# Query low parts in both halves of 128 rows, and the retention's distance table read per layer

## The chip, the cores and the metric

The kernel runs on one core of one Trainium2 chip. The metric is the device time of one execution in microseconds (us), as the median of several runs on the chip. Before the change it is 2534.63 us (three runs, 2533.9 to 2535.16).

## The reference, cut to what matters

One inference step of a two-layer backbone. 128 context tokens and 512 latent tokens go through the same weights. Each layer has one input projection, three token mixers side by side (differential attention, retention, multi-head latent attention, "MLA"), per-channel branch gates, an output projection and a squared-ReLU MLP.

```
z = h @ w_in                                     # 1024 -> 6848 columns
dq, dk = rmsnorm(d_q), rmsnorm(d_k)              # 8 half heads of 64 columns, rope on latents
s = dq . dk * 64**-0.5; p = softmax(s); a = p[0] - lam * p[1]; oa = a @ dv
rq, rk: 4 heads of 64 columns;  o = ((rq . rk) * decay(i - j)) @ rv + (rq * decay) @ state
mq = 128 columns without position + 64 with rope;  om = softmax(mq . mk * 192**-0.5) @ mv
merged = sum_i sigmoid(g_i) * (o_i @ w_branch[i]);  x = x + g1 * (merged @ w_out)
x = x + g2 * (relu(h2 @ w_up)**2 @ w_down)
```

Three products have a contraction of only 64: the differential scores, the retention scores and the rope part of the MLA scores. They are what the change touches.

## The kernel before, in words

All activations stand with features on the 128 partitions and T = 640 tokens along the free axis. Every fp32 operand of a matrix product is split in a high part and a low part of type fp32r (`splits`, the copy rounds to the high part and a subtraction leaves the low part), and a product is done as high*high + high*low + low*high (`mm3`).

For the products with 64 rows the high and low parts of the keys are stacked: rows 0 to 63 of a tile hold the high part and rows 64 to 127 the low part (for the second head of a pair the other way round). `split2` prepares the queries for them: `Q[:, g]` gets the high part twice, in both halves of the 128 rows, and the low part goes to `ql`, rows 0 to 63 for one head of the pair and 64 to 127 for the other. A score is then two matmuls: `Q[:, g]` against the stacked keys (128 rows, high*high + high*low), and `ql` against the high half of the keys alone (64 rows, low*high). The 64-row matmuls stand in `mla_scores` (`parts`), `diff_scores` (`parts`) and `ret_head` (`score`).

In `softmax_tile` a query tile of 128 against 640 keys is done as two halves of 320 columns: for each pair of operands first the one half, then the other. So the two 64-row matmuls of a tile follow each other, and a tile of 128 context keys has one. A retention tile has one of 512 or of 128 columns.

`ql` is a buffer of the pool "f" (7 buffers of [128, 640]). The distance table `dist` [128, 896] is loaded once at the start by a DMA that POOL issues, into a tile that lives throughout; `ret_head` makes the decay matrix from it on VectorE (DVE).

The order of the work is made by a planner in the kernel itself. The main line runs through the matrix products of a layer; preparations, softmax and value products are generators on side lanes. The planner holds an estimated clock for each engine (`est`), adds an estimated delay `LAT` from one engine's end to the next engine's start, and lets a generator go on when its estimated inputs are there. `yield from need(tag=n)` makes a generator wait until n buffers of a pool are free. The instructions are then issued in that order on each engine, so every constant of the planner can move the order on every engine. `pv_ctx` is the value product of the 128 context queries: transpose, split (ScalarE/ACT copy, DVE subtraction), three matmuls. `head_out` normalises a head's output; `down`, `gemm` and `gemm_half` are the large products, in groups of 12 or 24 matmuls of 320 columns.

Of the kernel before, what the change touches and what calls it, by code (L numbers as in the profile page):

```python
# [8 lines left out]
F32 = mybir.dt.float32  # L9
# [10 lines left out]
T = 640  # L20
# [9 lines left out]
def body(ctx, tc, ins, outs):  # L30
# [7 lines left out]
    dr = ctx.enter_context(tc.tile_pool(name="dr", bufs=1, space=DRAM))  # L38


    BUFS = {"s5": 20, "kc": 5, "vx": 2, "f": 7, "t": 3, "p": 5, "pt": 2, "w": 2, "stg": 2, "kr": 1, "m": 4,
            "o": 2, "ost": 2, "g": 3, "sc": 1, "tp": 2, "pv": 1}
    PS = ("g", "sc", "tp", "pv")
    avail = dict(BUFS)
    owner = {}
# [1 line left out]


    eng = dict(pe=0.0, a=0.0, v=0.0, p=0.0, sp=0.0, dma=0.0)
    LAT = dict(pe=0.16, a=0.11, v=0.09, p=0.04, dma=0.0)  # L50
    info = {}
    rel = {k: [0.0] * n for k, n in BUFS.items()}
    fin = [0.0]
# [271 lines left out]
            eng["pe"] += 0.1  # L325
            assert n < 3000

    nmm = [0]

    def mm(out, lhsT, rhs, start, stop, beside=False):  # L330
        n = rhs.free_size()
        k = 0.14 if lhsT.shape[0] == 64 else 0.0
        est("pe", 0.02 if beside else max(0.108, n / 2400.0 + 0.0135) + k if lhsT.dtype == F32R else max(0.222, n / 600.0),
            [lhsT, rhs], [out])
        nc.tensor.matmul(out, lhsT, rhs, start=start, stop=stop)  # L335

    def mm3(out, a, b, start, stop):
# [3 lines left out]
        mm(out, al, bh, False, stop)  # L341

    def tr(out, in_, k=128):
        est("pe", 0.109, [in_], [out])
        nc.tensor.transpose(out, in_, ident[0:k, 0:k])  # L345

# [3 lines left out]
    def c_act(in_):  # L350
        return (0.051 if inps(in_) else 0.093) + in_.free_size() / 1200.0
# [3 lines left out]

    def act(out, in_, func, **kw):
        w = [out] + ([kw["accum_out"]] if "accum_out" in kw else [])
        est("a", c_act(in_) + 0.15 * ("accum_out" in kw) + 0.06 * ("bias" in kw),
            [in_] + aps(*(kw.get(k) for k in ("bias", "scale"))), w)
        nc.scalar.activation(out=out, in_=in_, func=func, **kw)  # L360

# [66 lines left out]
    bones = const.tile([128, 128], F32R, name="bones")  # L428
    ropeC = const.tile([128, 512], F32, name="ropeC")
    ropeS = const.tile([128, 512], F32, name="ropeS")  # L430
    dist = const.tile([128, 896], F32, name="dist")
    posc = const.tile([128, 4], F32, name="posc")
    decb = const.tile([128, 2, 2, 2], F32, name="decb")
    lgn = const.tile([128, 2, 2], F32, name="lgn")
# [331 lines left out]
    def split2(src, Q, ql):  # L766

        for g in range(2):
            r = slice(64 * g, 64 * g + 64)
            yield "a"  # L770
            cp(Q[r, g], src[r])
            cp(Q[64 - 64 * g:128 - 64 * g, g], src[r])
            yield "v"
            tt(ql[r], src[r], Q[r, g], SUB, "vp")

    def splitk(src, keys, c0, c1, gs=(0, 1)):

# [43 lines left out]
    def params(brow, rows, rows2):  # L821
# [12 lines left out]
        dma(ropeC, ins["const_rope"][0], "p")  # L834
        dma(ropeS, ins["const_rope"][1], "p")
        dma(posc, ins["const_posc"], "p")
        dma(dist, ins["const_dist"], "p")
        yield from until(lambda: "r" in done)
        yield from written(rows2)
        yield from need(tp=1)  # L840
# [360 lines left out]
    def pv_ctx(P, v, dst):  # L1201
        yield from need(tp=1, pt=1)
        tp = bank("tp")
        tr(tp[:, 0:128], P[:, 0:128])
        free(P)
        pt = get("pt", [128, 2, 512], F32R)
        yield from splits(tp[:, 0:128], pt[:, 0, 0:128], pt[:, 1, 0:128])
        free(tp)
        yield from need(pv=1)
        pb = bank("pv")  # L1210
        mm3(pb[:, 0:128], v, (pt[:, 0, 0:128], pt[:, 1, 0:128]), True, True)
        free(pt)
        yield "a"
        dst(pb[:, 0:128])
        free(pb)
# [8 lines left out]
    def mla_scores(hd, qn, qr, ql, R, kn, kro, V):  # L1224
# [11 lines left out]
        def parts(qt):  # L1236
            q = slice(128 * qt, 128 * qt + 128)

            def at_(c0, c1):
                kh, kl = kn.hl(c0, c1)  # L1240
                rh, _, r2 = kro.slot(a, c0, c1)
                return [(qn[:, 0, q], kh), (qn[:, 0, q], kl), (qn[:, 1, q], kh), (qr[:, a, q], r2), (ql[pp, q], rh)]
            return at_

        for st_ in range(2):
# [32 lines left out]
    def diff_scores(l, hd, q, ql, R, k, V):  # L1278
# [4 lines left out]
        def qtile(qt):  # L1283
            n = T if qt < 4 else 128
            qc = slice(128 * qt, 128 * qt + 128)
            ps_, sms = [], []
            for g in range(2):
                def parts(c0, c1):
                    kh, _, k2 = k.slot(g, c0, c1)
                    return [(q[:, g, qc], k2), (ql[64 * g:64 * g + 64, qc], kh)]  # L1290
                p, sm = yield from softmax_tile(parts, 0 if qt < 4 else 640, n, R[:, 2 * qt + g:2 * qt + g + 1])
                ps_.append(p)
                sms.append(sm)
                if g == 0:
                    rs = small(2, "st2", 4)
                    est("v", 0.08, [sms[0]], [rs[:, 0:1]])
                    nc.vector.reciprocal(rs[:, 0:1], sms[0])
                    cp(ps_[0][:, 0:n], ps_[0][:, 0:n], scale=rs[:, 0:1])
            est("v", 0.08, [sms[1]], [rs[:, 1:2]])
            nc.vector.reciprocal(rs[:, 1:2], sms[1])  # L1300
            ts(rs[:, 1:2], rs[:, 1:2], lam[:, l:l + 1])
# [61 lines left out]
        heads[br] += 1  # L1363
        heads["n"] += 1

    def ret_head(l, hd, rq, rqs, rql, rks, V, r0s, flag):
        a = hd % 2
        pp = slice(64 * a, 64 * a + 64)
        pr = hd // 2
        vof = V.of(slice(128 * a, 128 * a + 128))  # L1370

        yield from need(s5=1)
        E = s5(F32, (128, 896))
        ts(E, dist, nlb[:, l, hd:hd + 1])
# [13 lines left out]
        free(dec)  # L1388
        if a == 1:
            free(rq)  # L1390
        yield from need(pt=1)
        qds = get("pt", [128, 2, 512], F32R)
        yield from splits(qd[:, 0:512], qds[:, 0], qds[:, 1])
# [7 lines left out]
        def score(jt):  # L1401
# [4 lines left out]
            i0 = 0 if jt < 4 else 512  # L1406
            sc = bank("tp")
            mm(sc[:, 0:n], rks[:, a, j0:j0 + 128], rqs[:, a, i0:i0 + n], True, False)
            mm(sc[:, 0:n], rks[pp, a, j0:j0 + 128], rql[0][pp, i0:i0 + n], False, True)
            A = get("p", [128, T])  # L1410
            yield "v"
            e0 = 384 - j0 if jt < 4 else 384
# [100 lines left out]
    def layer(l):  # L1513
# [70 lines left out]
        for p in range(2):  # L1584
# [16 lines left out]
            def rprep(rq=rq, rk=rk, rqs=rqs, rql=rql, rks=rks, pflag=pflag, f=fin[0]):  # L1601
# [30 lines left out]
            for a in range(2):  # L1632
                def go(a=a, p=p, rq=rq, rqs=rqs, rql=rql, rks=rks, V=V, x=pflag[a]):
                    yield from until(lambda: "qk" in x and "r0" in flag and "g" in done)
                    x["r0"] = 1
                    yield from ret_head(l, 2 * p + a, rq, rqs, rql, rks, V, flag["s"], x)
                pvq.append(go())
            yield from gates(gat(l, f"R{p}"))

# [126 lines left out]
        def dq_prep(hd, raw, dst, R, f):  # L1766
# [12 lines left out]
            yield "v"  # L1779
            yield from rope(raw, q)  # L1780
            free(q)
            yield from need(f=1)
            ql = get("f", [128, T], F32R)
            state["ql", hd] = ql
            yield from split2(raw, dst, ql)
            free(raw)
# [82 lines left out]
        def qkv(p):  # L1869
# [93 lines left out]
            def rr_prep(f):  # L1963
# [2 lines left out]
                t = tt_()  # L1966
                yield from rope(rr, t)
                free(t)
                yield from need(f=1)
                qlr.append(get("f", [128, T], F32R))  # L1970
                yield from split2(rr, qr, qlr[0])
                free(rr)
                yield ""
# [438 lines left out]
```

## Time and profile before

| | |
|---|---|
| median of the runs | 2534.63 us |
| the profiled execution, its own time | 2540.84 us |
| its span, first to last instruction | 2539.0 us |
| TensorE (PE) busy | 2470.7 us, 97% of the span |
| PE weight loads (PEld) | 2354.4 us, 93% |
| VectorE (DVE) busy | 1843.4 us, 73% |
| ScalarE (ACT) busy | 1077.9 us, 42% |
| GpSimd (POOL) busy | 99.2 us, 4% |
| mean granted TensorE clock | 0.988 |

A matmul's duration in the profile contains the pipeline's filling and draining, so the durations of neighbours overlap. What a matmul costs is the distance from its start to the start of the next one; the prediction works with these distances, which a timeline shows.

### The profile page before, as it was taken

The page shows a single profiled execution, that of the slowest core. Times are in us where ns is not written, and L with a number is a line of the kernel's source. Part 1 is how long each engine was busy: PE and PEld are TensorE (multiplying, and loading weights), DVE is VectorE, ACT ScalarE, POOL GpSimd, SP SyncE. Part 2 cuts the span into 40 slices and gives each one's busy share as a digit, 9 for nine tenths or more (in the row PEclk, how much of TensorE's full clock was granted, in tenths as well). Part 3 has the DMA queues.
Part 4 walks back from the last instruction along what each step waited for, and adds up shares of the span by engine and source line. Part 5 has one row for each costly group of instructions (what it writes and reads, how often), then busy time and mean ns, then how long its engine had stood idle before and what let it go on. Part 6 is the DMA issues. An engine that isn't in the chain of part 4 may idle for free.

```text
span 2539.0 us, 40871 instructions
## 1 busy us (share of the span) xinstructions
PE 2470.7 (97%) x16468; PEld 2354.4 (93%) x16468; DVE 1843.4 (73%) x3308; ACT 1077.9 (42%) x1976; POOL 99.2 (4%) x92
## 2 busy tenths in 40 slices
PE   7999999999999999999999999999999999999999
PEld 5998998989899999999999988988888999999999
DVE  6898878888789878786477787787888764344442
ACT  5564655656523412121254556564665352112122
POOL 2000000000100000000000000000001000000000
PEclk9998999999999999999999999999999999999999
DMA  9452321214365354554233322212233522222222
GB/s 308 128 155 70 99 68 51 83 41 127 106 234 172 113 172 155 162 164 124 75 110 95 95 70 79 70 57 77 63 101 130 177 67 75 76 75 75 75 75 84
DMA packets 333261, 274.99 MB, mean 108 GB/s; under 512 B 17454, under 2 KB 290304, under 8 KB 333072
## 3 DMA queue, kind: packets, MB, share of 16 engines
q1 hardware_dynamic: 332144, 271.04, 34.3%
q8 instruction: 130, 2.13, 0.3%
q0 software_dynamic: 928, 1.34, 0.2%
q14 instruction: 59, 0.48, 0.1%
HBM read 233.73 MB, written 33.36 MB: 105 GB/s over the span
## 4 chain that ended last, share of the span: by engine, by line
PE 74%; DVE 17%; ACT 4%; issue 3%; DMA 2%; SPq 0%; POOL 0%; DVEq 0%; ACTq 0%; POOLq 0%
PE g L335 63%; PE sc L335 4%; PE pv L335 4%; DVE w L377 3%; DVE f L377 2%; PE tp L335 2%; DVE s L377 2%; PE tp L345 1%; DVE p L364 1%; ACT t L360 1%; DVE t L377 1%; DVE t L364 1%; DVE st L1156 1%; DMA s<-in_w_mod_dram 1%; DMA p<-in_w_mod_dram 1%
## 5 line engine op out<-in xcount | busy, mean ns | idle before, releaser
L335 PE MATMUL g<-s,w 128*128 128x320 f32 (+1 forms) x12432 | 1939.3, 312 | 14.5 <-DVE w L377 9.1
L335 PEld LDWEIGHTS g<-s,w 128*128 128x128 f32 (+1 forms) x12432 | 1839.2, 188 | 44.6 <-issue 19.4
L377 DVE TENSOR_TENSOR w<-stg,w 128x1024 fp32r<-128x1024 f32 (+3 forms) x308 | 342.9, 1114 | 27.7 <-ACT w L392 23.8
L392 ACT ACTIVATE w<-stg 128x1024 fp32r<-128x1024 f32 (+2 forms) x182 | 166.5, 916 | 427.6 <-PE g L335 422.2
L364 DVE SCALAR_TENSOR_TENSOR s<-g,modT,s 128x320 f32<-128x320 f32 (+2 forms) x240 | 97.8, 435 | 201.8 <-PE g L335 201.4
L394 DVE CAST w<-stg 128x1024 fp32r<-128x1024 f32 (+3 forms) x139 | 89.7, 645 | 153.3 <-PE g L335 152.8
L360 ACT ACTIVATE f<-g 128x320 f32<-128x320 f32 x136 | 59.3, 438 | 332.8 <-PE g L335 332.8
L364 DVE SCALAR_TENSOR_TENSOR p<-p,cX,p 128x640 f32<-128x640 f32 (+2 forms) x238 | 190.2, 840 | 11.1 <-DMA p<-in_w_mod_dram 11.1
L360 ACT ACTIVATE t<-t 128x640 f32<-128x640 f32 (+2 forms) x204 | 148.0, 727 | 8.6 <-DVE t L364 2.2
L335 PE MATMUL g<-w,s 128*128 128x256 f32 x1080 | 139.5, 288 | 1.0 <-ACT s L392 0.5
L392 ACT ACTIVATE f<-g 128x320 f32<-128x320 f32 x176 | 75.8, 434 | 149.8 <-PE g L335 140.2
L335 PEld LDWEIGHTS g<-w,s 128*128 128x128 f32 x1080 | 134.9, 195 | 2.4 <-ACT s L392 0.8
L335 PE MATMUL pv<-pt,s 128*128 128x256 f32 (+2 forms) x624 | 120.5, 319 | 1.8 <-DVE pt L377 1.1
L1156 DVE TENSOR_REDUCE st<-sc 128x1 f32<-128x640 f32 (+1 forms) x120 | 85.5, 713 | 35.1 <-PE sc L335 34.6
L377 DVE TENSOR_TENSOR s<-f,s 128x320 fp32r<-128x320 f32 (+3 forms) x161 | 103.9, 650 | 6.9 <-ACT s L392 3.5
L335 PEld LDWEIGHTS pv<-pt,s 128*128 128x128 f32 x624 | 92.8, 196 | 11.9 <-issue 4.7
L335 PE MATMUL sc<-s,s 128*128 128x320 f32 x384 | 78.6, 327 | 7.2 <-ACT p L360 6.0
L360 ACT ACTIVATE p<-sc,st,rd 128x640 f32<-128x640 f32 (+1 forms) x80 | 63.8, 797 | 51.2 <-DVE st L384 50.9
L392 ACT ACTIVATE s<-f 128x320 fp32r<-128x320 f32 (+3 forms) x127 | 76.9, 606 | 12.2 <-DVE f L377 8.9
L377 DVE TENSOR_TENSOR pt<-tp,pt 128x512 fp32r<-128x512 f32 (+2 forms) x112 | 61.7, 552 | 18.0 <-ACT pt L392 16.7
L335 PEld LDWEIGHTS sc<-s,s 128*128 128x128 f32 x384 | 59.7, 193 | 13.9 <-ACT p L360 9.2
L392 ACT ACTIVATE pt<-tp 128x512 fp32r<-128x512 f32 (+2 forms) x80 | 40.2, 503 | 55.9 <-PE tp L345 55.0
(280 smaller groups left out, 2242.5 us busy)
## 6 DMA issues: line engine op xcount, KB each, us to landing
stg<-in_w_in_dram SPq DMA_DIRECT2D x106, 512.0 KB, 3.8
p<-in_w_mod_dram SPq DMA_DIRECT2D x120, 320.0 KB, 4.2
stg<-in_w_up_dram SPq DMA_DIRECT2D x64, 512.0 KB, 4.2
stg<-in_w_down_dram SPq DMA_DIRECT2D x64, 512.0 KB, 3.8
gdram<-f SPq DMA_DIRECT2D x56, 320.0 KB, 2.3
f<-gdram SPq DMA_DIRECT2D x56, 320.0 KB, 4.4
stg<-in_w_branch_dram SPq DMA_DIRECT2D x24, 512.0 KB, 3.4
s<-in_w_mod_dram SPq DMA_DIRECT2D x32, 256.0 KB, 6.6
```

Source lines behind the costliest of these rows:

```text
L335: nc.tensor.matmul(out, lhsT, rhs, start=start, stop=stop)
L345: nc.tensor.transpose(out, in_, ident[0:k, 0:k])
L360: nc.scalar.activation(out=out, in_=in_, func=func, **kw)
L364: nc.vector.scalar_tensor_tensor(out=out, in0=in0, scalar=scalar, in1=in1, op0=op0, op1=op1)
L377: (nc.vector if e == "v" else nc.gpsimd).tensor_tensor(out=out, in0=in0, in1=in1, op=op)
L392: nc.scalar.activation(out=out, in_=in_, func=AF.Copy, **({} if scale is None else {"scale": scale}))
L394: nc.vector.tensor_copy(out, in_)
L1156: nc.vector.reduce_max(out=nm, in_=sv, axis=AX.XY if n == T else AX.X, negate=True)
```

## The change

In words:

- `split2` writes the low part into a tile `ql` [128, 2, T] of a new pool "q" with one buffer. For each head of the pair the low part is computed into its own half of the rows and then copied into the other half (`cp`, which takes ACT or DVE).
- The second matmul of a score then has 128 rows: `ql[:, g]` (low part twice) against the stacked keys. It computes low*high + low*low. No 64-row score matmul is left.
- Pool "f" goes from 7 to 6 buffers. The constant tile `dist` is gone; instead `r0_load` reads the table in each layer into a tile of the pool "s5" (20 buffers), by a DMA on SP's queue, and it is freed after the layer's fourth retention head.
- The planner's constants: `LAT`, the cost of `accum_out`, the cost of a matmul (a table `TURN` by the kinds of the matmul before and of this one, in place of a surcharge of 0.14 for 64 rows), and a `yield ""` in `pv_ctx` between the split and the value product.

```diff
-    BUFS = {"s5": 20, "kc": 5, "vx": 2, "f": 7, "t": 3, "p": 5, "pt": 2, "w": 2, "stg": 2, "kr": 1, "m": 4,
-            "o": 2, "ost": 2, "g": 3, "sc": 1, "tp": 2, "pv": 1}
+    BUFS = {"s5": 20, "kc": 5, "vx": 2, "f": 6, "t": 3, "p": 5, "pt": 2, "w": 2, "stg": 2, "kr": 1, "m": 4,
+            "o": 2, "q": 1, "ost": 2, "g": 3, "sc": 1, "tp": 2, "pv": 1}
...
-    LAT = dict(pe=0.16, a=0.11, v=0.09, p=0.04, dma=0.0)
+    LAT = dict(pe=0.2, a=0.146, v=0.114, p=0.12, dma=0.0)
...
+    TURN = {(0, 1): 0.098, (1, 1): 0.105, (1, 0): 0.177, (2, 0): 0.09, (2, 1): 0.09}
...
-        k = 0.14 if lhsT.shape[0] == 64 else 0.0
...
+        cost = max(0.222, n / 600.0) if kind == 2 else max(0.108, n / 2400.0 + 0.0135) + TURN.get((turn[0], kind), 0.0)
...
-        est("a", c_act(in_) + 0.15 * ("accum_out" in kw) + 0.06 * ("bias" in kw),
+        est("a", c_act(in_) + 0.235 * ("accum_out" in kw) + 0.06 * ("bias" in kw),
...
-    dist = const.tile([128, 896], F32, name="dist")
...
-            tt(ql[r], src[r], Q[r, g], SUB, "vp")
+            tt(ql[r, g], src[r], Q[r, g], SUB, "vp")
+            yield "a"
+            cp(ql[64 - 64 * g:128 - 64 * g, g], ql[r, g])
...
-        dma(dist, ins["const_dist"], "p")
...
         free(tp)
+        yield ""
         yield from need(pv=1)
...
-                return [(qn[:, 0, q], kh), (qn[:, 0, q], kl), (qn[:, 1, q], kh), (qr[:, a, q], r2), (ql[pp, q], rh)]
+                return [(qn[:, 0, q], kh), (qn[:, 0, q], kl), (qn[:, 1, q], kh), (qr[:, a, q], r2), (ql[:, a, q], r2)]
...
-                    return [(q[:, g, qc], k2), (ql[64 * g:64 * g + 64, qc], kh)]
+                    return [(q[:, g, qc], k2), (ql[:, g, qc], k2)]
...
-            mm(sc[:, 0:n], rks[pp, a, j0:j0 + 128], rql[0][pp, i0:i0 + n], False, True)
+            mm(sc[:, 0:n], rks[:, a, j0:j0 + 128], rql[0][:, a, i0:i0 + n], False, True)
...
+            yield from need(s5=1)
+            flag["dist"] = s5(F32, (128, 896))
+            dma(flag["dist"], ins["const_dist"])
...
-                yield from need(f=1)
-                rql.append(get("f", [128, T], F32R))
+                yield from need(q=1)
+                rql.append(get("q", [128, 2, T], F32R))
```

The last four lines stand likewise in `dq_prep` and `rr_prep`.

The number of matmuls is the same before and after (16206 instructions). Their order moves nearly everywhere. Two places on PE:

**Second layer, the context queries of an MLA head** (`pv_ctx`; tp is the transpose of the probabilities, pv the value product, pt their split copy, g<-s,w a large product that fills in). Before:

```order
L335 MATMUL sc2594_17807<-s52453_16965,s52467_17009 128x320 x2
L335 MATMUL sc2594_17807<-s52453_16965,f2479_17066 128x320 x2
L345 MATMUL tp2595_17820<-ident_66,p2571_17672 128x128
L335 MATMUL g2584_17751<-s51949_13573,w2532_17482 128x320 x3
L335 MATMUL pv2598_17835<-pt2596_17822,vx2433_16848 128x128 x3
```

With the change:

```order
L338 MATMUL sc2589_17800<-s52455_16989,s52469_17033 128x320 x2
L338 MATMUL sc2589_17800<-s52455_16989,q2481_17094 128x320 x2
L349 MATMUL tp2590_17811<-ident_66,p2582_17759 128x128
L338 MATMUL g2578_17738<-s51957_13618,w2534_17507 128x320 x3
L338 MATMUL g2578_17738<-s51959_13627,w2534_17507 128x320 x3
L338 MATMUL g2578_17738<-s51961_13639,w2534_17507 128x320 x3
L338 MATMUL g2595_17840<-s51935_13507,w2559_17634 128x320 x3
L338 MATMUL g2595_17840<-s51939_13529,w2559_17634 128x320 x3
L338 MATMUL g2595_17840<-s51944_13558,w2559_17634 128x320 x3
L338 MATMUL pv2600_17857<-pt2591_17813,vx2435_16872 128x128 x3
```

The value product now stands 18 large matmuls behind its transpose, before it was 3. Over the 16 such places of the program, between 3 and 16 matmuls of any kind stood between before, and 9 to 27 stand there now.

**First layer, the last retention head** (tp is here the score, s,s its first matmul and f,s or q,s its second; pv<-pt the value product). Before, from the head's first score on:

```order
L335 MATMUL tp367_2540<-s5201_1410,s5202_1411 128x512
L335 MATMUL tp367_2540<-f235_1662,s5202_1411 128x512
L335 MATMUL g364_2525<-s582_431,w355_2419 128x320 x3
L335 MATMUL g364_2525<-s587_485,w355_2419 128x320 x3
L335 MATMUL g364_2525<-s594_541,w355_2419 128x320 x3
L335 MATMUL g364_2525<-s596_545,w355_2419 128x320 x3
L335 MATMUL tp371_2566<-s5201_1410,s5202_1411 128x512
L335 MATMUL tp371_2566<-f235_1662,s5202_1411 128x512
L335 MATMUL g364_2525<-s599_576,w355_2419 128x320 x3
L335 MATMUL pv366_2536<-pt369_2551,s5225_1583 128x512 x2
```

With the change:

```order
L338 MATMUL tp378_2584<-s5198_1400,s5199_1401 128x512
L338 MATMUL tp378_2584<-q276_1945,s5199_1401 128x512
L338 MATMUL tp381_2596<-s5198_1400,s5199_1401 128x512
L338 MATMUL tp381_2596<-q276_1945,s5199_1401 128x512
L338 MATMUL pv377_2580<-pt380_2592,s5227_1587 128x512 x2
L338 MATMUL pv377_2580<-pt380_2592,s5228_1588 128x512
L338 MATMUL tp384_2611<-s5198_1400,s5199_1401 128x512
L338 MATMUL tp384_2611<-q276_1945,s5199_1401 128x512
L338 MATMUL tp387_2621<-ones_67,t373_2574 128x1 x5
L338 MATMUL pv377_2580<-pt383_2603,s5227_1587 128x512 x2
```

The fifteen large matmuls that stood between this head's first scores and its first product are no longer there.

## Rows read from the trace of the kernel before

**Rows 1.** The page's first lines and its chain of work that ended last.
```profile
span 2539.0 us, 40871 instructions
...
PE 2470.7 (97%) x16468; PEld 2354.4 (93%) x16468; DVE 1843.4 (73%) x3308; ACT 1077.9 (42%) x1976; POOL 99.2 (4%) x92
...
PE 74%; DVE 17%; ACT 4%; issue 3%; DMA 2%; SPq 0%; POOL 0%; DVEq 0%; ACTq 0%; POOLq 0%
```

**Rows 2.** PE's groups by form: rows*columns, shape, count | busy, mean ns.
```profile
L335 PE MATMUL sc<-s,f 64*128 64x320 f32 x192 | 54.1, 362 | 0.0
L335 PE MATMUL tp<-f,s 64*128 64x512 f32 x32 | 16.2, 505 | 0.0
L335 PE MATMUL sc<-kc,f 64*128 64x128 f32 x24 | 7.8, 324 | 0.0
L335 PE MATMUL tp<-f,s 64*128 64x128 f32 x8 | 2.7, 342 | 0.0
```

**Rows 3.** Timeline of PE, a differential score tile: start us, duration us, engine, operation.
```profile
1805.56 0.46 PE L335 MATMUL sc<-s,s 128*128 128x320 f32 x2
1805.95 0.55 PE L335 MATMUL sc<-s,f 64*128 64x320 f32 x2
1806.43 0.33 PE L335 MATMUL pv<-pt,vx 128*128 128x128 f32 x1
```

**Rows 4.** Timeline of PE: 65 large matmuls in a row and their successor; 512 columns; 128 columns.
```profile
1487.81 9.70 PE L335 MATMUL g<-s,w 128*128 128x320 f32 x65
1497.34 2.92 PE L335 MATMUL g<-w,s 128*128 128x256 f32 x23
...
231.04 0.86 PE L335 MATMUL pv<-pt,s 128*128 128x512 f32 x3
231.74 0.39 PE L335 MATMUL tp<-s,s 128*128 128x512 f32 x1
...
256.45 0.78 PE L335 MATMUL g<-kc,w 128*128 128x128 f32 x6
257.06 1.97 PE L335 MATMUL g<-s,w 128*128 128x320 f32 x12
```

**Rows 5.** Timeline of PE: a retention score of 512 columns, a context score of 128.
```profile
227.14 0.40 PE L335 MATMUL tp<-s,s 128*128 128x512 f32 x1
227.47 0.49 PE L335 MATMUL tp<-f,s 64*128 64x512 f32 x1
227.89 2.02 PE L335 MATMUL g<-s,w 128*128 128x320 f32 x12
...
1946.42 0.22 PE L335 MATMUL sc<-kc,s 128*128 128x128 f32 x1
1946.57 0.32 PE L335 MATMUL sc<-kc,f 64*128 64x128 f32 x1
1946.83 1.58 PE L335 MATMUL g<-s,w 128*128 128x320 f32 x9
```

**Rows 6.** PE's weight loads by form: count | busy, mean ns | idle before, what ended it.
```profile
L335 PEld LDWEIGHTS g<-s,w 128*128 128x128 f32 x12336 | 1826.9, 189 | 42.0 <-issue 18.2 <-DVE w L377 10.9 <-DVE s L377 4.5
L335 PEld LDWEIGHTS sc<-s,f 64*128 64x128 f32 x192 | 28.7, 187 | 19.0 <-issue 19.0
L335 PEld LDWEIGHTS tp<-f,s 64*128 64x128 f32 x40 | 7.5, 188 | 12.7 <-issue 12.5
```

**Rows 7.** PE's waits: us in total, times, longest.
```profile
PE pv L335 <- DVE pt L377: 7.3, 8, 1.6
```

**Rows 8.** Copies and subtractions of 64 rows by form: count | busy, mean ns.
```profile
L392 ACT ACTIVATE s<-f 64x640 fp32r<-64x640 f32 x51 | 37.5, 736 | 6.8 <-DVE f L377 6.0
L394 DVE CAST s<-f 64x640 fp32r<-64x640 f32 x21 | 10.9, 519 | 0.4
L377 DVE TENSOR_TENSOR f<-f,s 64x640 fp32r<-64x640 f32 x25 | 20.4, 815 | 0.3
```

**Rows 9.** Stretches with many heads: busy us of PE, PEld, DVE, ACT, POOL, clock, DMA share.
```profile
450.00:620.00 170.00, 164.90 (x1117) 151.17 (x1116) 146.32 (x285) 103.92 (x204) 11.84 (x10) 1.00 0.26 79
1560.00:1960.00 400.00, 383.84 (x2547) 355.62 (x2546) 323.17 (x644) 224.02 (x437) 26.89 (x22) 0.98 0.26 81
```

**Rows 10.** Timeline, first layer's last retention head: DVE's work on one score, PE's last product.
```profile
228.23 0.68 DVE L377 TENSOR_TENSOR p<-tp,s 128x512 f32<-128x512 f32 x1
228.94 0.43 DVE L394 CAST pt<-p 128x512 fp32r<-128x512 f32 x1
229.41 0.69 DVE L377 TENSOR_TENSOR pt<-p,pt 128x512 fp32r<-128x512 f32 x1
...
245.96 0.95 PE L335 MATMUL g<-w,s 128*128 128x256 f32 x3
```

**Rows 11.** Timeline, second layer's last head: normalisation on PE, last split on DVE.
```profile
1960.99 0.75 PE L335 MATMUL sc<-s,ones 128*128 128x320 f32 x4
1961.58 23.63 PE L335 MATMUL g<-s,w 128*128 128x320 f32 x160
...
1970.81 0.82 DVE L377 TENSOR_TENSOR s<-o,s 128x640 fp32r<-128x640 f32 x1
```

**Rows 12.** DMA issues: KB each, median us to landing.
```profile
dist<-in_const_dist_dram POOLq DMA_DIRECT2D x1, 448.0 KB, 7.2
```

More of the change, by code (lines that the diff above doesn't have):

```diff
@@ L326, in drive @@
             assert n < 3000
-    nmm = [0]
+    TURN = {(0, 1): 0.098, (1, 1): 0.105, (1, 0): 0.177, (2, 0): 0.09, (2, 1): 0.09}
+    turn = [0]
     def mm(out, lhsT, rhs, start, stop, beside=False):
         n = rhs.free_size()
-        k = 0.14 if lhsT.shape[0] == 64 else 0.0
-        est("pe", 0.02 if beside else max(0.108, n / 2400.0 + 0.0135) + k if lhsT.dtype == F32R else max(0.222, n / 600.0),
-            [lhsT, rhs], [out])
+        kind = 2 if lhsT.dtype != F32R else int(lhsT.shape[0] == 64)
+        cost = max(0.222, n / 600.0) if kind == 2 else max(0.108, n / 2400.0 + 0.0135) + TURN.get((turn[0], kind), 0.0)
+        turn[0] = kind
+        est("pe", 0.02 if beside else cost, [lhsT, rhs], [out])
         nc.tensor.matmul(out, lhsT, rhs, start=start, stop=stop)
@@ L343, in tr @@
     def tr(out, in_, k=128):
+        turn[0] = 2
         est("pe", 0.109, [in_], [out])
@@ L1240, in at_ @@
                 kh, kl = kn.hl(c0, c1)
-                rh, _, r2 = kro.slot(a, c0, c1)
-                return [(qn[:, 0, q], kh), (qn[:, 0, q], kl), (qn[:, 1, q], kh), (qr[:, a, q], r2), (ql[pp, q], rh)]
+                r2 = kro.slot(a, c0, c1)[2]
+                return [(qn[:, 0, q], kh), (qn[:, 0, q], kl), (qn[:, 1, q], kh), (qr[:, a, q], r2), (ql[:, a, q], r2)]
             return at_
@@ L1288, in parts @@
                 def parts(c0, c1):
-                    kh, _, k2 = k.slot(g, c0, c1)
-                    return [(q[:, g, qc], k2), (ql[64 * g:64 * g + 64, qc], kh)]
+                    k2 = k.slot(g, c0, c1)[2]
+                    return [(q[:, g, qc], k2), (ql[:, g, qc], k2)]
                 p, sm = yield from softmax_tile(parts, 0 if qt < 4 else 640, n, R[:, 2 * qt + g:2 * qt + g + 1])
@@ L1364, in head_out, with ret_head @@
         heads["n"] += 1
-    def ret_head(l, hd, rq, rqs, rql, rks, V, r0s, flag):
+    def ret_head(l, hd, rq, rqs, rql, rks, V, r0s, dists, flag):
         a = hd % 2
@@ L1370, in ret_head @@
         vof = V.of(slice(128 * a, 128 * a + 128))
+        dist = dists["dist"]
         yield from need(s5=1)
@@ L1390, in ret_head @@
             free(rq)
+        if hd == 3:
+            free(dist)
         yield from need(pt=1)
@@ L1635, in go @@
                     x["r0"] = 1
-                    yield from ret_head(l, 2 * p + a, rq, rqs, rql, rks, V, flag["s"], x)
+                    yield from ret_head(l, 2 * p + a, rq, rqs, rql, rks, V, flag["s"], flag, x)
                 pvq.append(go())
@@ L1781, in dq_prep @@
             free(q)
-            yield from need(f=1)
-            ql = get("f", [128, T], F32R)
+            yield from need(q=1)
+            ql = get("q", [128, 2, T], F32R)
             state["ql", hd] = ql
@@ L1968, in rr_prep @@
                 free(t)
-                yield from need(f=1)
-                qlr.append(get("f", [128, T], F32R))
+                yield from need(q=1)
+                qlr.append(get("q", [128, 2, T], F32R))
                 yield from split2(rr, qr, qlr[0])
```

## The prediction

> **What bounds the kernel now.** The page's first lines come first: TensorE's matmuls fill 2470.7 of 2539.0 us, and the chain of work that ended last lies on PE for 74% [rows 1]. The reader is to see that nearly every microsecond PE's queue saves can shorten the run, so long as other engines keep pace. The busy time of PE says nothing on what a single matmul costs, because neighbours overlap; for that I read starts in the timeline. 65 large matmuls of 320 columns take 1497.34 - 1487.81 = 9.53 us, 0.147 us each; three of 512 columns take 0.70, 0.233 each; six of 128 columns 0.61, 0.10 each [rows 4].
>
> **The 64-row matmuls: -44.3 us.** There are 256 of them: 192 of 320 columns, 32 of 512, 24 + 8 of 128 [rows 2].
> - A tile of 2 x 320 columns: the last 128-row pair takes 0.39 us to the first 64-row matmul, that pair 0.48 us to whatever follows [rows 3]. Four plain matmuls would be 4 x 0.147 = 0.59. The surplus is 0.87 - 0.59 = 0.285, and there are 192 / 2 = 96 such tiles: 27.4 us.
> - A retention tile of 512: 0.33 + 0.42 = 0.75 [rows 5] against 2 x 0.233 = 0.466 [rows 4]: 0.29 x 32 = 9.3 us.
> - A tile of 128: 0.15 + 0.26 = 0.41 against 0.20, so 0.21 [rows 4, 5]. I take 0.24, between this and the retention's 0.29, for 24 + 8 = 32 tiles: 7.6 us.
>
> The sum is 44.3 us. A second view bounds it: before the 64-row weight loads PE's loader stood idle for 19.0 + 12.5 us in which it waited for nothing the profile shows, and another 18.2 us before large products, many of which follow a 64-row matmul [rows 6]. So at least 31.5 and at most about 50 us. With 128 rows in the second matmul every score is an ordinary pair, and I assume it costs 0.147, 0.233 and 0.10 like the others: the matmul count does not change, and the order listing has no 64-row score left.
>
> Here a rule of the Trainium skill speaks against the change. The rows show that a 64-row matmul and its successor take longer than two 128-row ones [rows 3, 5]. The Trainium skill, TensorE: Matmul & The Clock Gate, section "Why this matters for your kernels", says that a single matmul with K = 32 takes the same time as with K = 128, and gains only by running beside others. By it the term would be 0 in place of 44.3 us; the rows of this case don't agree, so it is a rival below with a small chance.
>
> **The context value products: -6 us.** PE waited 7.3 us, 8 times, for the split copy in front of a value product [rows 7]. In the order shown, 3 large matmuls (0.44 us) stood between transpose and product before, and 18 (2.6 us) stand there now; over all 16 places at least 9 matmuls, some 1.2 us. Not all eight waits need lie at these places, so I take 6 of 7.3; the ends are 0 and 7.3.
>
> **The new copies: 0.** 16 calls of `split2` (retention 2, differential 4, MLA 2 in each layer), each with two more copies of 64x640: 32 copies of 0.74 on ACT or 0.52 on DVE [rows 8], 17 to 24 us off PE. ACT is 42% busy and DVE 73% [rows 1], and what covers them is the large products of the main line. If that cover is gone, it is the rival on `ql` below.
>
> **One buffer for `ql`: 0.** Each head's (or pair's) low part must wait until the last score of the one before has been read. Then come, for two halves of the rows, two high copies, a subtraction and the new copy: 2 x (0.74 + 0.74 + 0.82 + 0.74) = 6.1 us if one engine does all in turn [rows 8], less where ACT and DVE share. In the changed order I counted the tightest handover, the first layer's last differential head: 39 large matmuls stand between the last read of the old tile and the first of the new, 39 x 0.147 = 5.7 us [rows 4], besides 15 value products and 7 transposes. So it is covered, barely.
>
> **The work that fills moves forward, and is missed in two places.**
> - First layer, last retention head: fifteen large matmuls have left the gaps between the scores (order shown). DVE spends 0.68 + 0.43 + 0.69 = 1.8 us on each of the four 512-column scores [rows 10], while PE has 0.70 for a product and 0.47 for a score [rows 4]: 0.6 us short per score. Before, this head took from 227.14 to 245.96, 18.8 us [rows 5, 10], and stood idle in it too. I take +2 us, with ends -1 (its five 64-row matmuls are counted above) and +6.
> - Second layer, end of the mixers: before, 10.0 us passed between the end of the last head's normalising matmuls and the end of its split on DVE, under 160 large matmuls [rows 11]. In the changed order 48 stand between, and 9 more before the head's own part is read: 57 x 0.147 = 8.4 us. That leaves +1.5 us, ends 0 and +4.
>
> **The table: 0.** A DMA of 448 KB lands after 7.2 us [rows 12]. Once from POOL's queue becomes twice from SP's; in the first layer it is issued ahead of the first retention head by the whole first projection, in the second likewise behind the state's buffers. It occupies one of 20 "s5" tiles, and the order shows no head held back for it.
>
> **The planner's constants** move thousands of instructions. I give them 0 with plus or minus 8 us: PE's whole idle time is 2539.0 - 2470.7 = 68 us [rows 1], most of it in other waits that could shrink or grow.
>
> **Sum.** -44.3 - 6 + 2 + 1.5 = -46.8 us. The profiled execution took 2540.84 us, 6.2 above the median of 2534.63; the same difference against the median gives **2488 us**, -1.8%.
>
> **The rivals.**
> - *DVE becomes the bound among the heads.* It has 146.3 of 170 us in the first layer's stretch and 323.2 of 400 in the second's [rows 9]. If the 22 us saved per layer all came out of such a stretch, the first would be 148 long with 146.3 plus up to 8 copies x 0.52 = 150.5 us of DVE work. For: the numbers touch. Against: the second layer has 77 us to spare, and only part of the heads lies there. Price: half of the 64-row term, 22 us, so 2510.
> - *`ql` serialises the heads, and the run gets slower.* The place is the handover of the "q" buffer, 15 of them; it decides from 46.8 / 15 = 3.1 us of idle PE each. With all 6.1 us bare it is +92 us, 2580. For: one buffer, and planned cover of the same size as the chain. Against: the count of 39 matmuls at the tightest place.
> - *The price is not the rows'.* If a low-part matmul costs what it costs for another reason (its operand, its place behind the pair), 128 rows change nothing: 2534.6 - 6 + 3.5 = 2532. Against: 128-row matmuls of the same tiles run at plain distances within a tile, and the idle loader stands before 64-row forms alone, 0.10 us each over 192 [rows 6].
>
> **How the numbers follow.** Forecast 0.83, DVE 0.10, no change 0.04, slower 0.03. The range: down to 50 + 7.3 + 8 saved with 3.5 lost, 2473; up to the DVE case with a little on it, 2513. About 0.2% (5 us) is what a measurement of this kernel can tell from no change. Faster by more than that: the first two cases, 0.93 plus a little of the third, less what the planner's order could spoil: 0.94. Same 0.03, slower 0.03.
>
> **What would show it.** In the changed profile: no 64-row score group; a low-part pair with its successor at 0.147 us distances; the loader's idle time by "issue" down by over 30 us; PE's wait for pt before pv under 2 us; DVE's busy time up by some 10 us at most while the span falls, so its share rises to some 75%; one stretch near 200 to 240 us with PE idle behind DVE. I am wrong if 128-row low parts keep distances over 0.2 us, if waits on "q" tiles or on ACT copies take 20 us or more, or if DVE's share in the head stretches reaches 95%.

## The result, and the profile after

The changed kernel takes 2490.94 us (median of four runs, 2487.88 to 2494.18), beside 2534.27 for the kernel before on the same chip. The ratio is 0.9832, interval 0.9814 to 0.9849: 43.3 us or 1.7% faster. The forecast was 2488 us within 2473 to 2513. The total is right. But the planner's constants and the side costs of the new data path, both put at 0, were worth some 10 to 24 us each, with opposite signs; only the runs below show it.

The profiled execution took 2491.77 us. The page's first lines and its chain of work that ended last, to be read against [rows 1]:

```profile
span 2489.4 us, 40869 instructions
...
PE 2414.8 (97%) x16468; PEld 2352.9 (95%) x16468; DVE 1866.3 (75%) x3374; ACT 1069.3 (43%) x1954; POOL 77.3 (3%) x79
...
PE 74%; DVE 17%; ACT 4%; issue 2%; DMA 2%; SPq 1%; POOL 0%; DVEq 0%; ACTq 0%; POOLq 0%
```

PE remains the bound at the same 74% of the chain: its busy time fell by 55.9 us with the same 16468 matmuls. DVE has 66 instructions more, ACT 22 and POOL 13 fewer. That is more than 32 copies would bring: the planner also handed work from ACT and POOL to DVE.

PE's groups by form, the ones that answer to [rows 2]; the last number is idle time before the group and what ended it:

```profile
L338 PE MATMUL sc<-s,s 128*128 128x320 f32 x384 | 77.4, 323 | 14.7 <-ACT p L364 13.1 <-DVE t L368 1.2
L338 PE MATMUL pv<-pt,s 128*128 128x256 f32 x480 | 77.0, 286 | 5.9 <-DVE pt L381 5.7
L338 PE MATMUL sc<-s,q 128*128 128x320 f32 x192 | 44.5, 314 | 0.0
L338 PE MATMUL tp<-q,s 128*128 128x512 f32 x32 | 12.8, 400 | 0.0
L338 PE MATMUL pv<-pt,vx 128*128 128x128 f32 x48 | 8.4, 270 | 1.4 <-DVE pt L381 1.4
```

PE's weight loads by form, beside [rows 6]:

```profile
L338 PEld LDWEIGHTS g<-s,w 128*128 128x128 f32 x12336 | 1833.9, 189 | 21.7 <-DVE s L381 7.6 <-DVE w L381 3.2 <-ACT f L364 2.8
L338 PEld LDWEIGHTS sc<-s,q 128*128 128x128 f32 x192 | 33.0, 192 | 0.0
```

The low parts (`sc<-s,q`, `tp<-q,s`) now have 128 rows. The 19.0 us in which the loader stood before them without a visible reason are gone, and "issue" is no longer among the large products' first three releasers, where it was first with 18.2.

PE's waits: us in total, times, longest.

```profile
PE sc L338 <- ACT p L364: 13.6, 9, 4.0
...
PE pv L338 <- DVE pt L381: 7.6, 19, 1.3
```

The wait for the split copy pt, 7.3 us in 8 pieces before [rows 7], is 7.6 in 19 now. At the context products (`pv<-pt,vx`) it is down to 1.4 us, but it has appeared in front of the pair products (`pv<-pt,s`, 5.7 us). Before, the two forms had:

```profile
L335 PE MATMUL pv<-pt,s 128*128 128x256 f32 x480 | 79.0, 295 | 1.1 <-DVE pt L377 1.1
L335 PE MATMUL pv<-pt,vx 128*128 128x128 f32 x48 | 11.3, 296 | 6.4 <-DVE pt L377 6.3
```

The wait for a score buffer that ACT's exponential still reads leads the list with 13.6 us; it was 9.4. All of PE's waits in this view add up to 69.4 us, before to 63.2: the waits as a whole have grown.

The two places from which filling work was moved away, in the timeline of PE, beside [rows 5, 10, 11]: the first layer's last retention head, and the end of the second layer's mixers.

```profile
225.04 0.40 PE L338 MATMUL tp<-s,s 128*128 128x512 f32 x1
225.28 0.40 PE L338 MATMUL tp<-q,s 128*128 128x512 f32 x1
225.51 0.39 PE L338 MATMUL tp<-s,s 128*128 128x512 f32 x1
...
238.60 0.56 PE L338 MATMUL g<-w,s 128*128 128x256 f32 x3
...
1928.81 0.75 PE L338 MATMUL sc<-s,ones 128*128 128x320 f32 x4
1929.39 8.67 PE L338 MATMUL g<-s,w 128*128 128x320 f32 x58
1938.78 1.43 PE L338 MATMUL g<-s,w 128*128 128x320 f32 x8 [0.71 <-DVE s L381]
```

A 512-column score now stands at 0.24 and 0.23 us distances, the plain ones of [rows 4]. The head lasts 238.60 - 225.04 = 13.6 us; it lasted 18.8. Three things left it: fifteen large products (15 x 0.147 = 2.2 us), the surplus of five 64-row matmuls (4 x 0.29 + 0.24 = 1.4), and ten small `tp<-bones` products (236.00 - 234.77 = 1.2), which now stand ahead of it. Before:

```profile
234.77 1.36 PE L335 MATMUL tp<-bones,p 128*128 128x2 f32 x10 [2.22 <-DVE p L377]
236.00 1.63 PE L335 MATMUL pv<-pt,s 128*128 128x512 f32 x3
```

So PE's idle time within the head hardly changed: its busy time is 15.91 of 18.82 us in that stretch before and 11.02 of 13.56 now, which leaves 2.9 and 2.5 us. The tail waits 0.71 us behind 58 matmuls.

### The profile page after: what moved, and what is told of

Same layout as the page of the kernel before. It is cut to its first block, busy times and chain, and to the rows that moved or that the text cites. A ratio compares the mean times of both kernels' runs of the same rounds, so it can differ in the third digit from the quotient of the medians.

```text
span 2489.4 us, 40869 instructions
## 1 busy us (share of the span) xinstructions
PE 2414.8 (97%) x16468; PEld 2352.9 (95%) x16468; DVE 1866.3 (75%) x3374; ACT 1069.3 (43%) x1954; POOL 77.3 (3%) x79
## 4 chain that ended last, share of the span: by engine, by line
PE 74%; DVE 17%; ACT 4%; issue 2%; DMA 2%; SPq 1%; POOL 0%; DVEq 0%; ACTq 0%; POOLq 0%
PE g L338 64%; PE sc L338 4%; PE pv L338 3%; DVE s L381 2%; DVE w L381 2%; PE tp L338 2%; DVE p L368 1%; DVE f L381 1%; PE tp L349 1%; ACT t L364 1%; DMA s<-in_w_mod_dram 1%; DVE t L368 1%; DVE pt L381 1%; DVE st L1160 1%; SPq L160 1%
## 5 line engine op out<-in xcount | busy, mean ns | idle before, releaser
L381 DVE TENSOR_TENSOR w<-stg,w 128x1024 fp32r<-128x1024 f32 (+3 forms) x314 | 341.3, 1087 | 30.5 <-ACT w L396 26.3
L396 ACT ACTIVATE w<-stg 128x1024 fp32r<-128x1024 f32 (+3 forms) x183 | 172.2, 941 | 407.8 <-PE g L338 402.2
L396 ACT ACTIVATE s<-f 128x320 fp32r<-128x320 f32 (+3 forms) x109 | 64.1, 590 | 14.0 <-DVE f L381 12.0
L364 ACT ACTIVATE t<-f 128x640 f32<-128x640 f32 x82 | 59.9, 732 | 2.5 <-PE tp L338 1.4
```

Of the source, the lines that this page charges most:

```text
L381: (nc.vector if e == "v" else nc.gpsimd).tensor_tensor(out=out, in0=in0, in1=in1, op=op)
L396: nc.scalar.activation(out=out, in_=in_, func=AF.Copy, **({} if scale is None else {"scale": scale}))
```

## The experiments

All ratios are against the kernel before on the same chip. "Own order" means that the planner planned anew.

### What the rows alone are worth, and the planner's constants

**e1_low64** keeps the changed kernel's order, copies, buffers and table, but the low-part matmuls have 64 rows again:

```diff
-        kind = 2 if lhsT.dtype != F32R else int(lhsT.shape[0] == 64)
+        kind = 2 if lhsT.dtype != F32R else 0
...
-                    return [(q[:, g, qc], k2), (ql[:, g, qc], k2)]
+                    return [(q[:, g, qc], k2), (ql[64 * g:64 * g + 64, g, qc], kh)]
```

(likewise in `mla_scores` and `ret_head`).

> The changed kernel with every instruction in the same order, but the low-part matmul reads 64 rows again (low part of one half, high keys only), so the product low*low is left out and the copies of the low part are made and not read. Theory (a 64-row matmul and its successor cost 0.09 to 0.2 us more each): the whole 44 us come back, 2535 us, and the loader's idle time by issue before 64-row forms returns to about 33 us. Rival (the number of rows does not matter, the gain came from the new order): 2491 us within 5. Between the two: the order gave part of it.

Measured: 2533.4 us, ratio 0.9998 (0.9988 to 1.0008). So in this order the rows are worth 2533.4 - 2490.9 = 42 us, beside 44.3 forecast. The two profiled executions agree: e1's span is 37.5 us longer (2526.9 beside 2489.4), although its waits are 13.2 us shorter (56.2 in all) and only some 5.5 us more went to the lower clock (mean 0.986 beside 0.988; the span times what the mean lacks to 1, idle time included, is 35.4 beside 29.9). That leaves an estimate of some 45 us of work. The loader's idle time is back, in the weight loads by form:

```profile
L338 PEld LDWEIGHTS sc<-s,q 64*128 64x128 f32 x192 | 28.7, 187 | 18.8 <-issue 18.8
```

But it also says that everything else in the change, taken together in this order, is worth nothing; the sum had -2.5 us there, for the waits.

**e2_oldplan** is the changed kernel with the old `LAT`, the old cost of `accum_out`, an empty `TURN` and no added yield, in its own order; **e3_noyield** takes the yield alone away, also in its own order.

```diff
-    LAT = dict(pe=0.2, a=0.146, v=0.114, p=0.12, dma=0.0)
+    LAT = dict(pe=0.16, a=0.11, v=0.09, p=0.04, dma=0.0)
...
-    TURN = {(0, 1): 0.098, (1, 1): 0.105, (1, 0): 0.177, (2, 0): 0.09, (2, 1): 0.09}
+    TURN = {}
...
-        yield ""
```

> The changed kernel with 128 rows, one ql buffer and the table per layer, but the planner's constants of before (LAT, accum_out, no table TURN, no extra cost for any matmul) and without the yield in pv_ctx. Theory as predicted (the constants and the yield are worth the 6 us of waits before the context value products): about 2497 us, with PE's waits for pt before the context value products back to 5 to 7 us. Rival (the planner's part is nothing, or even a loss): 2491 us or under. Second rival (the planner's part carried the result): over 2510 us.

> The changed kernel without the one yield in pv_ctx, the other constants as changed. Theory: the yield alone moved the context value products away from their transposes, so the wait there returns, 4 to 6 us, 2496 us. Rival (larger LAT alone moves them): wait under 2 us and 2491 us.

Measured: e2 2501.84 us, 0.9879 (0.9864 to 0.9893), 11 us slower than the change; e3 2491.24 us, 0.9836 (0.9822 to 0.9851), no difference. The constants matter for the time, the yield by itself does not. Which of the constants does it was not tried.

The yield does matter for the wait that it is aimed at. Without it the context products wait 14.5 us in place of 1.4:

```profile
L338 PE MATMUL pv<-pt,vx 128*128 128x128 f32 x48 | 11.8, 308 | 14.5 <-DVE pt L381 13.4 <-ACT pt L396 0.7 <-DVE pt L398 0.3
```

Yet the time is the same, and so is the sum of PE's waits (69.5 us beside 69.4): the wait for the exponential, for one, is 8.0 in place of 13.6. A wait that goes at one place is not yet time that the run saves.

**e7_newplan_before** is the other half: the kernel before, 64 rows and all, with the planner's new constants, `TURN` and the yield, and nothing else.

```diff
-    LAT = dict(pe=0.16, a=0.11, v=0.09, p=0.04, dma=0.0)
+    LAT = dict(pe=0.2, a=0.146, v=0.114, p=0.12, dma=0.0)
...
-        k = 0.14 if lhsT.shape[0] == 64 else 0.0
...
+        cost = max(0.222, n / 600.0) if kind == 2 else max(0.108, n / 2400.0 + 0.0135) + TURN.get((turn[0], kind), 0.0)
```

> The kernel of before (64-row low parts in pool f, table loaded once) with the planner's constants of the change, TURN among them, and the yield in pv_ctx. Undoing them on the changed kernel cost 11 us. Theory (the planner's part is worth the same on either kernel and the parts add up): 11 us faster than before, 2523 us. Rival (the constants pay only where no 64-row matmuls stand): 2531 to 2536 us.

Measured: 2509.71 us, 0.9904 (0.9889 to 0.9919): 24.5 us faster, more than either theory had. PE's waits in this kernel:

```profile
PE g L337 <- DVE s L380: 5.6, 10, 1.2
PE g L337 <- DVE w L380: 4.8, 4, 1.7
...
PE pv L337 <- DVE pt L380: 3.2, 5, 1.1
...
PE sc L337 <- ACT p L363: 2.7, 5, 0.8
```

The wait for pt fell from 7.3 to 3.2 us here, that for the exponential from 9.4 to 2.7, and all of PE's waits together (the rows of this view summed) from 63.2 to 46.7 us. The mean granted clock rose from 0.988 over 2539.0 us to 0.991 over 2508.5, which is 30.5 and 22.6 us lost to it. These two, 16.5 and 7.9 us, make up most of the 30.5 by which the two spans differ. With e2 this makes a table of two by two, in us:

| | old constants | new constants |
|---|---|---|
| data path of before | 2534 | 2510 (e7) |
| data path of the change | 2502 (e2) | 2491 (the change) |

The rows, copies, buffer and table together bring 32 us under the old constants, 19 under the new; the constants bring 24 on the old data path and 11 on the new. The parts don't add up to the whole; the likely reason, which is argued only, is that each order leaves other waits. Beside the 42 us of the rows, the rest of the new data path thus costs some 10 us under the old constants and some 23 under the new.

### Where the 24 us went

From e7 to e1 the matmuls have the same rows. What differs is the copies, one wide buffer for `ql`, the table per layer, and an order planned as if the low parts were ordinary matmuls. It costs 2533.4 - 2509.7 = 24 us. The last of these belongs to e1 alone: in the changed kernel the low parts are ordinary matmuls, as its order assumes. So the 24 us are not all a cost that the change itself bears.

**e13_oneq** is e7 with `ql` in a pool of one buffer (and "f" at 6), without copies; its own order.

```diff
-    BUFS = {"s5": 20, "kc": 5, "vx": 2, "f": 7, "t": 3, "p": 5, "pt": 2, "w": 2, "stg": 2, "kr": 1, "m": 4,
-            "o": 2, "ost": 2, "g": 3, "sc": 1, "tp": 2, "pv": 1}
+    BUFS = {"s5": 20, "kc": 5, "vx": 2, "f": 6, "t": 3, "p": 5, "pt": 2, "w": 2, "stg": 2, "kr": 1, "m": 4,
+            "o": 2, "q": 1, "ost": 2, "g": 3, "sc": 1, "tp": 2, "pv": 1}
```

> The kernel of before with the planner's new constants (64-row low parts, table loaded once, no copies), and ql [128, 640] in a pool of its own with one buffer, with 6 in pool f: the one ql buffer alone. Without it this kernel takes 2509.7 us; with it and with the copies and the table per layer 2533.4. Theory (the one buffer holds back each head's preparation and gives back most of the planner's gain): 2524 to 2531 us. Rival (one buffer is covered, and the table per layer, the s5 tile or the copies are what costs): 2508 to 2514 us.

Measured: 2512.12 us, 0.991 (0.9897 to 0.9924), beside 2509.71: the one buffer by itself is not it.

**e8_low64_nocopy** is e1 in the same order without the 32 copies, which the 64-row matmuls don't read; **e4_copy2** is the changed kernel in the same order with each copy made twice. The lines are e4's, where `cp` also returns the engine that it took:

```diff
-            cp(ql[64 - 64 * g:128 - 64 * g, g], ql[r, g])
+            lo2 = ql[64 - 64 * g:128 - 64 * g, g]
+            if cp(lo2, ql[r, g]) == "a":
+                nc.scalar.activation(out=lo2, in_=ql[r, g], func=AF.Copy)
+            else:
+                nc.vector.tensor_copy(lo2, ql[r, g])
```

> The kernel with 64-row low parts in the changed order, and without the 32 copies of the low part that it does not read (low*low left out, as there); every other instruction in the same order. Doubled copies cost 9 us. Theory (the cost is linear, a copy in the head stretches delays what is queued behind it on ACT or DVE): the first copies cost about as much, so this is 9 us faster than with them, 2524 us. Rival (one copy fits in the gaps and only the second does not): 2531 to 2534 us.

> The changed kernel with each of the 32 copies of the low part made twice on the same engine, all else in the same order; 32 copies of 0.5 to 0.75 us more. Theory (the copies lie beside PE's work): 2491 to 2494 us. Rival (DVE or ACT binds among the heads): plus 10 to 24 us, 2501 to 2515.

Measured: e8 2529.36 us, 0.9977 (0.9967 to 0.9987), 0.2% below e1 and between its two theories; e4 2500.34 us, 0.9872 (0.9858 to 0.9887), 9.4 us above the change. So a copy is not free: 32 of them cost some 5 us (4 by the medians, 5 by the ratios), a second set 9. Where the 5 us lie isn't shown: the profiled executions of e1 and e8 happen to take the same time (2529.27 and 2529.11 us). For the second set, PE's waits sum to 75.2 us in place of 69.4, and the mean granted clock is 0.984 in place of 0.988. The changed kernel's copies by form (the first from ACT, the second from DVE; the last number is the idle time before them):

```profile
L396 ACT ACTIVATE q<-q 64x640 fp32r<-64x640 f32 x20 | 14.8, 738 | 19.3 <-DVE q L381 19.2
L398 DVE CAST q<-q 64x640 fp32r<-64x640 f32 x12 | 5.9, 488 | 0.4
```

The work itself, 20.7 us, is as forecast. But the 20 copies on ACT left that engine idle for 19.2 us, waiting for DVE's subtraction, and what stands behind a copy in ACT's order of work waits with it. Most of that cost PE nothing: without the copies (e8) the run gained 5 us, not 19. Nor is it the whole of the matter, since e4's second copies wait for no other engine and cost 9.

**e9_dmadup** lets a DMA on SP's queue make the second half, so that neither ACT nor DVE waits; its own order:

```diff
-            yield "a"
-            cp(ql[64 - 64 * g:128 - 64 * g, g], ql[r, g])
+            yield ""
+            dma(ql[64 - 64 * g:128 - 64 * g, g].bitcast(F32), ql[r, g].bitcast(F32))
```

> The changed kernel with the second half of the low part filled by a DMA on SP's queue (160 KB, 32 of them; such DMAs landed after 2.7 us in the trace before) in place of the copy on ACT or DVE; the planner sees it and the order moves. Theory (the copies cost some 5 us by the time they take from ACT and DVE): 2484 to 2489 us. Rival (the longer latency of the one buffer's handover, or the new order, eats it): 2490 to 2500 us.

Measured: 2486.6 us, 0.9811 (0.9797 to 0.9826). That is 4 us below the change, as much as e8 gave, though the two intervals overlap. PE's wait for the exponential is 6.6 us in place of 13.6. It has the lowest median of all versions measured here.

What a wait for the exponential does, in the changed kernel's timeline (ACT's exponential `p<-sc` frees the score buffer):

```profile
596.10 3.24 PE L338 MATMUL g<-s,w 128*128 128x320 f32 x21
...
597.40 0.82 DVE L1160 TENSOR_REDUCE st<-sc 128x1 f32<-128x640 f32 x1
...
598.26 0.21 DVE L388 TENSOR_SCALAR st<-st,rd 128x1 f32<-128x1 f32 x1
...
600.88 1.51 ACT L364 ACTIVATE t<-t 128x640 f32<-128x640 f32 x2
...
602.29 0.87 ACT L364 ACTIVATE p<-sc,st,rd 128x640 f32<-128x640 f32 x1
...
603.30 0.90 PE L338 MATMUL sc<-s,s 128*128 128x320 f32 x2 [3.96 <-ACT p L364]
```

The row maximum is ready at 598.5; the exponential begins at 602.29, behind other operations on ACT, and no large product stands in PE's order between the last of the 21 and the next score. None of those operations is a copy of `ql`, and e8, without the copies, still waits 10.4 us for the exponential beside 11.1 in e1: the copies are at most a small part of such waits. PE idles 3.96 us and then runs slower: by stretches (busy us of PE, PEld, DVE, ACT, POOL; then granted clock, DMA share),

```profile
585.00:595.00 10.00, 8.73 (x58) 8.20 (x56) 9.73 (x18) 5.88 (x12) 0.46 (x1) 1.00 0.93 320
595.00:605.00 10.00, 5.60 (x31) 5.37 (x32) 9.80 (x15) 8.19 (x13) 0.00 (x0) 0.83 0.20 65
605.00:615.00 10.00, 7.57 (x38) 7.17 (x38) 6.30 (x14) 4.45 (x11) 1.42 (x2) 0.66 0.31 101
615.00:625.00 10.00, 9.94 (x72) 9.65 (x71) 8.64 (x19) 6.84 (x15) 0.00 (x0) 1.00 0.24 85
```

The mean granted clock falls from 1.00 to 0.83 and 0.66, between the levels of 2.4 and 1.2 GHz, and a pair of score matmuls takes 0.70 us to the next (603.30 to 604.00 in the same timeline) in place of 0.29. So at this place a wait costs PE twice.

**e11_q1** and **e11_q2** are the changed kernel with pools "t" 2 and "kc" 4 (to make room) and one or two buffers for `ql`; **e5_q1** has "f" 5, "p" 4 and one buffer. All three in their own order.

```diff
-    BUFS = {"s5": 20, "kc": 5, "vx": 2, "f": 6, "t": 3, "p": 5, "pt": 2, "w": 2, "stg": 2, "kr": 1, "m": 4,
-            "o": 2, "q": 1, "ost": 2, "g": 3, "sc": 1, "tp": 2, "pv": 1}
+    BUFS = {"s5": 20, "kc": 4, "vx": 2, "f": 6, "t": 2, "p": 5, "pt": 2, "w": 2, "stg": 2, "kr": 1, "m": 4,
+            "o": 2, "q": 2, "ost": 2, "g": 3, "sc": 1, "tp": 2, "pv": 1}
```

> The changed kernel with 2 tiles in pool t and 4 in pool kc, one ql buffer: the partner of the next run, which needs this room. 2495 to 2560 us, since fewer buffers in f and p cost 69 us.

> As its partner with two ql buffers. Theory (the one buffer's handover is covered by large products): within 4 us of its partner. Rival (one buffer serialises the heads): 5 us or more faster than its partner.

> The changed kernel with 5 buffers in pool f and 4 in pool p, one ql buffer: the partner of the next run, which needs this room. Expected within 5 us of the changed kernel, 2488 to 2498.

Measured: e11_q1 2535.46 us, 1.0005 (0.9996 to 1.0015); e11_q2 2509.44, 0.9901 (0.9886 to 0.9916); e5_q1 2559.77, 1.0097 (1.0082 to 1.0112). Two buffers beside the change's other pools need 203.3 KB per partition of the on-chip memory, and 199.3 are free, so two other pools had to shrink. Under these tight pools the second buffer is worth 26 us. PE's first waits with one buffer,

```profile
PE sc L338 <- ACT p L364: 37.3, 19, 7.3
PE tp L338 <- DVE t L381: 20.7, 4, 7.8
```

and with two:

```profile
PE sc L338 <- ACT p L364: 22.6, 14, 7.3
PE tp L338 <- DVE t L381: 11.0, 3, 5.2
```

The mean granted clock is 0.975 and 0.983. No wait of PE names a `q` tile, here or in the changed kernel. That the late second half of `ql` appears as a wait for the exponential is argued, not shown. How much of the 26 us holds with the change's own pools isn't shown either. No version of e5_q1 with two buffers was run, so it tells of the pools alone: 69 us for one buffer less in each of "f" and "p", where at most 5 or so were expected.

So of the 24 us the copies are some 5. The rest, about 19, lies in e1's order, planned for another price of the low parts, with its one buffer held longer and the table among the "s5" tiles, and the runs don't separate these. The profiles of e7 and e1 say where it lies: PE's waits sum to 46.7 and 56.2 us, +9.5, and the mean granted clock is 0.991 over 2508.5 us and 0.986 over 2526.9, that is 22.6 and 35.4 us lost to it, +12.8; the two spans differ by 18.4.

### What makes a 64-row matmul dear

**e6_low64x2** is e1 with each 64-row softmax matmul made once more behind the tile (216 more; the low part is added twice), in the same order.

```diff
-                mm(sc[:, b, 0:m], *ops[i], i == 0, i == last)
+                mm(sc[:, b, 0:m], *ops[i], i == 0, False)
+        for b, m, ops in halves:
+            nc.tensor.matmul(sc[:, b, 0:m], *ops[last], start=False, stop=True)
```

> The kernel with 64-row low parts in the changed order, and each 64-row matmul of the softmax tiles made twice (the low part is added twice, so the scores change): four 64-row matmuls in a row per 640-key tile, 192 + 24 more in all. Theory (each 64-row matmul pays, because its weight load is not hidden behind the one before): 0.25 us each, 216 x 0.25 = 54 us more, 2587 us. Rival (the price is paid at the change between 128 and 64 rows and back, and not between two of the same kind, as the Trainium skill's page TensorEngine Tiling (Array Packing), Key Properties, has it for a change of mode): 192 x 0.147 + 24 x 0.10 = 31 us more, 2564 us.

Measured: 2549.94 us, 1.0061 (1.0046 to 1.0076), 16 us above e1, well below the 54 of the theory that each matmul pays. An MLA tile in the timeline of PE, of e1, of the change and of e6:

```profile
304.61 1.34 PE L338 MATMUL sc<-s,s 128*128 128x320 f32 x8
305.88 0.56 PE L338 MATMUL sc<-s,q 64*128 64x320 f32 x2
306.37 0.85 PE L338 MATMUL g<-s,w 128*128 128x320 f32 x4
```

```profile
300.85 1.34 PE L338 MATMUL sc<-s,s 128*128 128x320 f32 x8
302.03 0.46 PE L338 MATMUL sc<-s,q 128*128 128x320 f32 x2
302.32 0.89 PE L338 MATMUL g<-s,w 128*128 128x320 f32 x5
```

```profile
304.32 1.34 PE L338 MATMUL sc<-s,s 128*128 128x320 f32 x8
305.58 0.56 PE L338 MATMUL sc<-s,q 64*128 64x320 f32 x2
305.98 0.46 PE L1157 MATMUL sc<-s,q 64*128 64x320 f32 x2
306.36 0.85 PE L338 MATMUL g<-s,w 128*128 128x320 f32 x4
```

From the tile's first matmul to its successor: 1.76 us with two 64-row matmuls, 1.47 with none (10 x 0.147), 2.04 with four. The third and fourth add 0.28 us, 0.14 each: the plain price. So a 64-row matmul costs what one of 128 rows costs, and the surplus of about 0.29 us is paid once per stay (a run of 64-row matmuls between 128-row ones), at the changes from 128 to 64 rows and back. The weight loads of e6 say the same of all 96 tiles: the loader stands idle for 18.8 us in all before the first pairs and for 0.0 before the second.

```profile
L338 PEld LDWEIGHTS sc<-s,q 64*128 64x128 f32 x192 | 28.7, 187 | 18.8 <-issue 18.8
L1157 PEld LDWEIGHTS sc<-s,q 64*128 64x128 f32 x192 | 32.2, 187 | 0.0
```

The Trainium skill, TensorEngine Tiling (Array Packing), section "Key Properties", says that changing the tiling mode drains TensorE; the trace agrees with a price per change, 0.29 us for there and back at 320 columns, though no row shows the draining itself.

The whole run grew by 16 us and not by the 192 x 0.147 + 24 x 0.10 = 31 of the added work. Most of the rest is the clock: e6's mean is 0.990 over 2546.8 us, 25.5 us lost, beside 35.4 in e1, and its waits sum to 54.5 us beside 56.2. By this estimate 31 - 9.9 - 1.7 leaves some 19 us, and the two spans differ by 19.9. Why the clock is higher in e6 isn't shown.

## Why the prediction was right, and which steps were not

- **The 64-row matmuls, -44.3: right.** 42 us by e1, and the tile measured 0.29 us shorter, as the start distances said. Reading distances in place of durations is what made it right: the durations of the forms fell by only 9.6 us (54.1 to 44.5) for the tiles and 3.4 (16.2 to 12.8) for the 512-column scores. The rule that was set against it, that of the Trainium skill, TensorE: Matmul & The Clock Gate, section "Why this matters for your kernels" (a single matmul with few rows costs what 128 rows cost), agrees with the second pair of e6, 0.14 us each. It still missed the price, which lies in the change between row counts.
- **The context value products, -6: right at their place (6.4 us to 1.4, the forms' idle time), wrong for PE.** "PE's wait for pt before pv under 2 us" failed: 7.6. The wait moved to the pair products, and all waits together rose from 63.2 to 69.4 us where the sum had -2.5. The step took a wait that goes for time saved; e3 waits 13 us longer at the same place and takes the same time as the change. With the new constants alone (e7) the wait for pt is 3.2.
- **"The new copies: 0": undersized.** The 20.7 us of work were right, the cover was not: some 5 us by e8. The step took an engine's low busy share (ACT 42%) and the large products for cover; e4 shows that a second set, without any wait of its own, costs 9.4. That what stands behind a copy pays is the likely way, and argued only.
- **"One buffer for `ql`: 0" and "The table: 0":** the buffer alone, without copies, holds (e13, 2 us). With copies and tight pools it is 26 (e11), though no wait of PE names a `q` tile. Copies, buffer, table and the order that goes with them cost 24 us together by e1 and e7, part of it perhaps e1's order alone, where the sum had none. The table alone was not tried.
- **"The planner's constants: 0 with plus or minus 8": wrong by size.** On the old data path they give 24.5 us, three times the bound. The step said that most of PE's 68 us of idle time lay in other waits that could shrink or grow, and then took a small part of it without a reason. On the new data path they are worth 11.
- **The two places behind the moved work:** the retention head did not lose 2 us but idles about 0.4 less; the tail waits 0.7, not 1.5. Both inside their ends.
- **DVE as the bound: did not come.** Its busy time rose by 23 us, over the "some 10 at most", and it has 89% and 86% of the two stretches with many heads, below the 95% set:

```profile
450.00:610.00 160.00, 149.01 (x1061) 145.03 (x1059) 142.17 (x274) 102.15 (x195) 8.95 (x9) 0.97 0.30 91
1530.00:1930.00 400.00, 387.71 (x2720) 378.72 (x2719) 345.79 (x692) 228.01 (x447) 25.66 (x18) 0.98 0.29 90
```

So the main term was right by itself, and that the sum came out right as well is luck: the constants (-24.5 us on the old data path, -11 on the new, in place of 0) and the side costs of the new data path (+23 under the new constants, +10 under the old, in place of 0) cancelled, and nothing in the prediction foresaw it.

## What to carry to other kernels

Price a matmul with fewer rows by start distances over the whole stay, from the last matmul ahead of it to the first behind it: group such matmuls together or fill them up to 128 rows, since here each change cost and the matmul itself cost nothing extra. When a change brings planner constants along with a data path, measure each alone and both together; a right total can hide two wrong terms. Don't book a wait that disappears as time saved before you know where it goes. Don't take an engine's low busy share for cover of a small copy: double the copy and look. A DMA queue with nothing urgent behind can be the better place, though the 4 us of e9 lie within the intervals.

## What the runs showed of the hardware that was not expected

- Two 64-row matmuls behind two others cost 0.14 us each, like 128 rows; there and back between the two row counts costs about 0.29 us (e1 beside the change, 320 columns).
- A wait of 3.96 us of PE was followed by a granted clock of 0.66 in the next ten us, which also hold a wait of 2.43 us. One buffer less in both "t" and "kc" cost 45 us (e11_q1), in both "f" and "p" 69 us (e5_q1), with a mean granted clock of 0.975 in both against 0.988.
